# The second half of an output projection: four pairs in phases on four banks, their first phase laced with the first half's last pair

## The chip, the cores and the metric

The kernel runs on one core of one Trainium2 chip. The metric is the device time of one execution in microseconds (us), as the median of several runs; a profiled execution of the same program gives the trace that is read below.

## The reference, cut to what matters

The program is a trunk of two layers on 256 tokens of width 2048, all in float32. Each layer has one input projection, two kinds of attention (8 heads each), one output projection, and a gated feed-forward block, with a norm and a residual around each half.

```python
def hybrid_mixer(h, layer, w_in, w_o, ...):
    proj = h @ w_in                       # 2048 -> 12 blocks of 512 columns
    ...                                   # 8 stick-breaking heads, 8 differential heads
    mix = jnp.concatenate([o_sb.reshape(b, s, SB_WIDTH),
                           o_d.reshape(b, s, DIFF_V_WIDTH)], axis=-1)
    return mix @ w_o                      # (256 x 2048) @ (2048 x 2048): the change is here

for l in range(DEPTH):                    # DEPTH = 2
    h = rms_norm(x, pre_mix_norm[l])
    m = hybrid_mixer(h, l, w_in[l], w_o[l], ...)
    x = x + rms_norm(m, post_mix_norm[l])
    h = rms_norm(x, pre_ffn_norm[l])
    f = swiglu(h, w_gate[l], w_up[l], w_down[l])
    x = x + rms_norm(f, post_ffn_norm[l])
```

## The kernel before

**A product and its weights.** Every float32 weight block is split in two: ScalarE writes its rounded part `hi` (`activation ... Copy`), VectorE the rest `lo = w - hi`. A product of 128 tokens x 128 rows of K with 512 columns is three matmuls of 512 columns: `hi` by the rounded tokens, `lo` by the rounded tokens, `hi` by the tokens' rest (function `product`, and the same in `unit`). Weights arrive by DMA into `raw` (four buffers of 128 x 1024), in one order that is fixed when the kernel is built (`weight_order`); the split goes into `hi` and `lo` (six buffers each). What is to be split next stands in a list of jobs, which `weights` and `feed_jobs` work off a few jobs ahead of the product.

**A pair.** K is handled in pairs of 128-row blocks (`kp` = 0 to 7). The output projection has four blocks of 512 columns (`c` = 0 to 3), done as a first half (c = 0, 1) and a second half (c = 2, 3). With the two token blocks, two K blocks and two column blocks, one pair is a 2 x 2 by 2 x 2 product of blocks. There are three ways to do it:

- plain (`unit`): 8 products, 24 matmuls, two column blocks one after the other; VectorE makes one `lo` of 128 x 1024 for each column block;
- in seven (`mixed_weights`, `seven_products`): 7 products, 21 matmuls, after sums of weights (`t2`, `t3`, `t4`, ...) and sums of tokens (`pair_forms`, `token_sums`: tiles `sh`, `sl`); four of the products go into banks of their own (`p1`, `p6`, `p7`, `q5`), which are added to the results later, so eight banks are in use;
- phased (`phased`): the same 7 products for several pairs, but first the products `g0`, `t1`, `t2`, `t3` of all pairs into the four result banks, then four operations of VectorE and two copies of ScalarE that mix the banks, then `g1`, `b22`, `t4` of all pairs on top. Four banks are enough. The weight sums are made from three loads: `u1` (128 x 512 per pair), `first` (128 x 1024 per pair: a job that makes `g0` and `t1`, a job that makes `t2` and `t3`), `g1` (128 x 512 per pair, two pairs in a tile: the job for `g1`, then one for `b22` and `t4` of each pair). `first_part` and `second_part` do these jobs.

**The order.** TensorE (PE), VectorE (DVE) and ScalarE (ACT) each run their instructions in an order that is set when the kernel is built: a scheduler sets it from priorities (`tc.high_priority`, `tc.issue_after` pull things forward or hold them back), and in `passage`, the bridge from the output projection to the feed-forward block, it is written by hand. In the first half of the output projection pairs 4, 5, 6 are phased (`O_PHASED`) and pairs 7, 0, 2, 1, 3 plain (`O_PLAIN`). In the second half pairs 4 and 5 (`O_SEVEN`) are done in seven, with weights in buffers of their own (`V`), the other six plain; the last ones (`LATE_O[-1]`, `LAST_O`) are done in `passage`, one token block after the other, between the steps of the norm. While the plain pairs of the first half run, the attention's last heads are finished, and x and the norm's gain are loaded.

## Time and profile before

| | |
|---|---|
| time, median of 3 runs (lowest to highest) | 2169.59 us (2169.15 to 2169.59) |
| profiled execution: time, span of its instructions | 2169.97 us, 2168.3 us |
| PE busy, share of the span, instructions | 2154.1 us, 99%, 9896 |
| DVE busy, share, instructions | 1986.9 us, 92%, 2767 |
| ACT busy, share, instructions | 1434.7 us, 66%, 2163 |
| output projection: start of the first and of the last matmul, layer 1 of 2 | 297.8 us, 389.3 us |
| output projection: start of the first and of the last matmul, layer 2 of 2 | 1375.9 us, 1467.4 us |

Times count from the span's start. In the rows below a line number with an L is a line of the kernel, an arrow leads from the inputs to the output of an instruction, and brackets hold the time that the engine sat idle before it and what it waited for. DVE and matmul rows overlap a little: what an engine can do in a stretch is read from the distance of the starts, not from the durations. The lines of the changed kernel are numbered differently from those of the kernel before: of `first_part`, L354, L356 and L360 are now L352, L354 and L358; `lo = w - hi` (L346) is now L344; of `second_part`, L375 is now L373; the mixing in `phased`, L1222 to L1230, is now L1230 to L1238; the norm's gain, L703, is now L701.

### The profile page before, as it was taken

The numbers are of one execution on the slowest core, as the hardware profiler recorded it, in microseconds if no ns is written. First come the engines' busy times: TensorE is split into PE (matmuls) and PEld (weight loads), VectorE is DVE, ScalarE is ACT, GpSimd is POOL, SyncE is SP. The second block draws the span as 40 slices with busy tenths as digits, with TensorE's granted clock in tenths as the row PEclk, the third lists the DMA queues.
The fourth block names the chain that finished last, engine by engine and source line by source line (L and its number), as shares of the span: only waits on it lengthen the run. The fifth ranks groups of instructions, "written<-read, shape, count | busy, mean of one in ns | idle before, by whom it ended". The sixth has DMA issues, their size and how long they took to land.

```text
span 2168.3 us, 28898 instructions
## 1 busy us (share of the span) xinstructions
PE 2154.1 (99%) x9896; PEld 1773.9 (82%) x9896; DVE 1986.9 (92%) x2767; ACT 1434.7 (66%) x2163; POOL 241.1 (11%) x234
## 2 busy tenths in 40 slices
PE   9999999999999999999999999999999999999998
PEld 7888888888888888888878888888888888888887
DVE  7898987899999999999897989888999999999997
ACT  7667775766766666666575777757566666666664
POOL 1110000021221220000020100000112222100000
PEclk9999999999999999999999999999999999999999
DMA  8554556497887776777465555555978878767683
GB/s 295 183 193 157 173 175 246 156 309 235 243 264 224 233 240 226 227 228 253 147 207 188 176 182 175 182 204 190 308 218 269 242 224 241 230 218 245 201 270 99
DMA packets 143155, 470.43 MB, mean 217 GB/s; under 512 B 16272, under 2 KB 17296, under 8 KB 142496
## 3 DMA queue, kind: packets, MB, share of 16 engines
q1 hardware_dynamic: 124832, 436.03, 57.9%
q0 software_dynamic: 17600, 32.02, 9.0%
q8 instruction: 77, 1.26, 0.2%
q14 instruction: 70, 0.57, 0.1%
q10 hardware_dynamic: 576, 0.54, 0.1%
HBM read 460.14 MB, written 8.39 MB: 216 GB/s over the span
## 4 chain that ended last, share of the span: by engine, by line
PE 91%; DVE 4%; ACT 2%; DMA 2%; issue 1%; DVEq 0%; ACTq 0%
PE c L1311 21%; PE in L1255 5%; PE in L1254 5%; PE in L1256 5%; PE dn L1634 4%; PE dn L1631 4%; PE dn L1632 4%; PE p L1255 3%; PE p L1256 3%; PE c L1255 3%; PE c L1254 3%; PE c L1256 3%; PE p L1254 3%; DVE lo L346 2%; PE o L693 2%; PE o L695 2%
## 5 line engine op out<-in xcount | busy, mean ns | idle before, releaser
L346 DVE TENSOR_TENSOR lo<-raw,hi 128x1024 fp32r<-128x1024 f32 (+1 forms) x512 | 594.6, 1179 | 62.1 <-ACT hi L407 35.8
L407 ACT ACTIVATE hi<-raw 128x1024 fp32r<-128x1024 f32 x440 | 450.9, 1057 | 107.2 <-DMA raw<-in_weights_in_turn_dram 71.9
L1311 PE MATMUL c<-hi,xF 128*128 128x512 f32 x1344 | 364.3, 392 | 0.5 <-DVE xF L608 0.5
L1311 PEld LDWEIGHTS c<-hi,xF 128*128 128x128 f32 x1344 | 249.9, 188 | 52.6 <-DVE xF L608 1.3
L301 POOL DMA_DIRECT2D T<-in_weights_in_turn_dram x122 | 106.9, 876 | 1364.8 <-DMA T<-in_weights_in_turn_dram 279.2
L1311 PE MATMUL c<-lo,xF 128*128 128x512 f32 x672 | 207.5, 390 | 0.0
L322 ACT ACTIVATE Th<-T 128x512 fp32r<-128x512 f32 x122 | 77.2, 632 | 182.8 <-DVE T L333 180.6
L322 ACT ACTIVATE Th<-G 128x1024 fp32r<-128x1024 f32 x122 | 129.0, 1058 | 77.0 <-DVE G L334 75.8
L1631 PE MATMUL dn<-hi,jh 128*128 128x512 f32 x416 | 162.1, 390 | 0.0
L1632 PE MATMUL dn<-lo,jh 128*128 128x512 f32 x416 | 161.9, 389 | 0.0
L324 DVE TENSOR_TENSOR Tl<-G,Th 128x1024 fp32r<-128x1024 f32 x122 | 148.8, 1220 | 11.6 <-ACT Th L322 11.6
L407 ACT ACTIVATE hi<-G 128x1024 fp32r<-128x1024 f32 x122 | 129.0, 1057 | 41.6 <-DMA G<-in_weights_in_turn_dram 21.3
L324 DVE TENSOR_TENSOR lo<-T,hi 128x1024 fp32r<-128x1024 f32 x122 | 152.1, 1247 | 0.0
L334 DVE TENSOR_TENSOR G<-G,T 128x1024 f32<-128x1024 f32 x122 | 148.6, 1218 | 1.8
L1311 PEld LDWEIGHTS c<-lo,xF 128*128 128x128 f32 x672 | 126.0, 188 | 26.4
L346 DVE TENSOR_TENSOR lo<-G,hi 128x1024 fp32r<-128x1024 f32 x106 | 129.2, 1219 | 10.5 <-ACT hi L407 10.5
L322 ACT ACTIVATE hi<-T 128x1024 fp32r<-128x1024 f32 x122 | 128.1, 1050 | 12.0 <-PE c L1256 9.1
L1634 PE MATMUL dn<-hi,jl 128*128 128x512 f32 x416 | 128.2, 389 | 0.0
L1254 PE MATMUL in<-hi,xT 128*128 128x512 f32 x309 | 122.2, 398 | 0.8 <-ACT hi L1008 0.8
L1255 PE MATMUL in<-lo,xT 128*128 128x512 f32 x309 | 120.9, 392 | 1.4 <-DVE lo L346 1.4
L1256 PE MATMUL in<-hi,xT 128*128 128x512 f32 x309 | 120.3, 390 | 0.0
L1254 PE MATMUL in<-hi,xI 128*128 128x512 f32 x285 | 114.2, 401 | 0.0
(462 smaller groups left out, 5064.3 us busy)
## 6 DMA issues: line engine op xcount, KB each, us to landing
raw<-in_weights_in_turn_dram SPq DMA_DIRECT2D x510, 512.0 KB, 4.9
T<-in_weights_in_turn_dram SPq DMA_DIRECT2D x122, 512.0 KB, 5.3
G<-in_weights_in_turn_dram SPq DMA_DIRECT2D x122, 512.0 KB, 5.4
T<-in_weights_in_turn_dram POOLq DMA_DIRECT2D x122, 256.0 KB, 5.6
u<-in_weights_in_turn_dram SPq DMA_DIRECT2D x36, 256.0 KB, 5.7
V<-in_weights_in_turn_dram SPq DMA_DIRECT2D x8, 512.0 KB, 4.6
away_ffn<-x SPq DMA_DIRECT2D x8, 512.0 KB, 7.2
xd<-away_ffn SPq DMA_DIRECT2D x8, 512.0 KB, 8.7
```

What stands on the lines that cost most here:

```text
L322: nc.scalar.activation(h, w, AF.Copy)
L324: newest_rest[i] = nc.vector.tensor_tensor(out=l, in0=w, in1=h.bitcast(F32), op=ALU.subtract)
L334: nc.vector.tensor_tensor(out=g, in0=g, in1=t2.unsqueeze(1).to_broadcast([P, 2, CW]), op=ALU.add)
L346: rests.append(nc.vector.tensor_tensor(out=lo, in0=src, in1=hi.bitcast(F32), op=ALU.subtract))
L407: nc.scalar.activation(hi, raw, AF.Copy)
L1254: nc.tensor.matmul(a, sh, hi, start=first, stop=False, skip_group_check=open_sums[0])
L1255: nc.tensor.matmul(a, sh, lo, start=False, stop=False, skip_group_check=open_sums[0])
L1256: return nc.tensor.matmul(a, sl, hi, start=False, stop=last, skip_group_check=open_sums[0])
L1311: nc.tensor.matmul(a, stat[part], w[j][:, kk, :], start=first and kk + n == 0, stop=last and kk == 1 and n == 2)
L1631: nc.tensor.matmul(accs[c, t], sh, hi[:, kk, :], start=first, stop=False, skip_group_check=open_sums[0])
L1632: nc.tensor.matmul(accs[c, t], sh, lo[:, kk, :], start=False, stop=False, skip_group_check=open_sums[0])
L1634: nc.tensor.matmul(accs[c, t], sl, hi[:, kk, :], start=False, stop=last, skip_group_check=open_sums[0])
```

## The change

In the second half pairs 4, 5, 6 and 7 are phased (`O_LATER`), on four banks, in place of 4 and 5 in seven on eight banks; pairs 0, 1, 2, 3 are plain there, 1, 2 and 3 of them in `passage`. The first half's last plain pair, pair 3, is moved into the first phase of the second half: after the first products of pair 4 its column block 0, after those of pair 5 its column block 1. So two sets of four banks are open at once. The token sums of pairs 4 and 5 are still those made for the first half; those of pairs 6 and 7 are made once more (`later`), after two of the plain pairs of the first half. In `passage` the adding of the extra banks goes (one copy of ACT, eight additions of DVE).

```diff
-LATE_O = (6, 4, 0, 1, 5, 2)
-LAST_O = (3, 7)
-O_SEVEN = (4, 5)
+O_LATER = (4, 5, 6, 7)
+LATE_O = (0, 1)
+LAST_O = (2, 3)
...
-    def queue_phase(key, name, l, kps, cc):
+    def queue_phase(key, name, l, kps, cc, between=()):
+        between = list(between)
         for some in in_twos(kps):
             roles[queue(*((name, l, 2 * kp + 1, cc[1]) for kp in some))] = "u1", key, some
             for kp in some:
                 roles[queue(*((name, l, 2 * kp, c) for c in cc))] = "first", key, (kp,)
+                if between:
+                    between.pop(0)()
...
-        order_o = [(c, kp) for kp in O_PLAIN for c in (0, 1)]
-        order_o += [(c, kp) for kp in LATE_O for c in (2, 3)] + [(c, kp) for c in (2, 3) for kp in LAST_O]
+        for kp in O_PLAIN[:-1]:
+            for c in (0, 1):
+                queue_o(c, kp)
+        queue_phase(("o2", l), "w_o", l, O_LATER, (2, 3), [lambda c=c: queue_o(c, O_PLAIN[-1]) for c in (0, 1)])
+        for c, kp in [(c, kp) for kp in LATE_O for c in (2, 3)] + [(c, kp) for c in (2, 3) for kp in LAST_O]:
+            queue_o(c, kp)
...
+    def upper_room(key, name):          # where u1 of the new phase lies: in mg's second half, then in V's two buffers
+        if key[0] != "o2":
+            return late_room([P, 2, CW], name)
+        return spare_rooms.pop(0) if spare_rooms else mix_pool[0].tile([P, 2, CW], F32, tag="v", bufs=2, name=name)
...
-        for two in in_twos(kps[:-2]):
+        for two in in_twos(kps[:alone]) if not between else [(kp,) for kp in kps[:alone]]:
             for names in (("g0", "t1"), ("t2", "t3")):
                 for kp in two:
                     products(kp, *names)
+            if two[-1] in others:
+                place, work = others[two[-1]]
+                work()
...
         with tc.manual_schedule(engines=by_hand):     # passage
             last_units(0, (0, 1))
-            nc.scalar.copy(m[0], p1)
-            nc.vector.tensor_tensor(out=m[1], in0=p6, in1=m[0], op=ALU.subtract)
-            ...
+            if extra:                                 # None for the output projection now
+                ...
...
+            if n == 4:
+                for (later, tags, bufs) in zip(O_LATER[2:], (("ah", "al"), ("w", "w")), (1, 3)):
+                    forms[later] = pair_forms(pool, pool, bufs, mix, later, f"later{l}", tags=tags)
...
+        phased(got, forms, mix, ("o2", l), O_LATER, [w[0], w[1], w[0]], [lambda c=c: end_of_half(c) for c in (0, 1)])
         for kp in LATE_O[:-1]:
-            ...                                       # plain, or seven_products for O_SEVEN
+            for c in (2, 3):
+                unit({t: accs[c, t] for t in range(NT)}, mix, plan[l]["o"][c, kp], kp, range(NT), False, False)
```

The order of the instructions is the same in both kernels up to the last plain pairs of the first half; it differs from there to the end of `passage`, in each layer, on PE, DVE, ACT and the DMA queue of SyncE (SP), and nowhere else. In names such as `lo115_0`, 115 is the place of the load in the weights' order and 0 or 1 the job; `o0_2_1` is layer 0, column block 2, token block 1.

DVE where the second half begins, layer 0, before:

```order
L800 SCALAR_TENSOR_TENSOR mix_sb0_1_1_0_3385<-oT_ps_sb0_1_1_3387,gains_89,mix_sb0_1_1_0_3385 128x256
L346 TENSOR_TENSOR lo114_3382<-raw114_3379,hi114_3381 128x1024
L800 SCALAR_TENSOR_TENSOR mix_sb0_1_1_1_3386<-oT_ps_sb0_1_1_3387,gains_89,mix_sb0_1_1_1_3386 128x256
L346 TENSOR_TENSOR lo115_3411<-raw115_3408,hi115_3410 128x1024
L346 TENSOR_TENSOR lo116_3429<-V116_3426,hi116_3428 128x1024
L328 TENSOR_TENSOR V117_3450<-V116_3426,V117_3450 128x512
L324 TENSOR_TENSOR lo117_3453<-V117_3450,hi117_3452 128x1024
```

DVE at the same place now, from the plain tile `lo114` (pair 3, column block 0) to the second of pair 6's two first tiles:

```order
L344 TENSOR_TENSOR lo114_3413<-raw114_3410,hi114_3412 128x1024
L798 SCALAR_TENSOR_TENSOR mix_sb0_1_1_0_3416<-oT_ps_sb0_1_1_3418,gains_89,mix_sb0_1_1_0_3416 128x256
L352 TENSOR_TENSOR raw115_3439<-raw115_3439 128x512
L798 SCALAR_TENSOR_TENSOR mix_sb0_1_1_1_3417<-oT_ps_sb0_1_1_3418,gains_89,mix_sb0_1_1_1_3417 128x256
L354 TENSOR_TENSOR mg_o0_1_1_2956<-mg_o0_1_1_2956,raw115_3439 128x512
L352 TENSOR_TENSOR raw118_3488<-raw118_3488 128x512
L344 TENSOR_TENSOR lo115_0_3442<-raw115_3439,hi115_0_3441 128x1024
L344 TENSOR_TENSOR lo115_1_3466<-mg_o0_1_1_2956,hi115_1_3465 128x512
L358 TENSOR_TENSOR raw115_3439<-raw115_3439,mg_o0_1_1_2956 128x512
L344 TENSOR_TENSOR lo116_3475<-raw116_3472,hi116_3474 128x1024
L344 TENSOR_TENSOR lo115_1_3466<-raw115_3439,hi115_1_3465 128x512
L354 TENSOR_TENSOR u1_117_0_3484<-u1_117_0_3484,raw118_3488 128x512
```

Between two whole `lo` tiles there now stand additions of 128 x 512 for the phased pairs, and the addition that waits for `raw118` stands ahead of `lo115_0`.

DVE in the middle of the second half, layer 0, before (pair 5 in seven, after plain tiles):

```order
L346 TENSOR_TENSOR lo121_3538<-raw121_3535,hi121_3537 128x1024
L346 TENSOR_TENSOR lo122_3565<-V122_3562,hi122_3564 128x1024
L328 TENSOR_TENSOR V123_3580<-V122_3562,V123_3580 128x512
L324 TENSOR_TENSOR lo123_3583<-V123_3580,hi123_3582 128x1024
L333 TENSOR_TENSOR V123_3580<-V123_3580 128x512
L334 TENSOR_TENSOR V122_3562<-V122_3562,V123_3580 128x1024
```

DVE now, between the last product of the first phase and the first tile of the last phase (`lo120_0`, which PE reads for `g1`):

```order
L701 TENSOR_TENSOR mg_o0_0_0_2953<-o0_1_0_2950,gpost_mix0_3222 128x512
L701 TENSOR_TENSOR mg_o0_1_0_2954<-o0_1_1_2952,gpost_mix0_3222 128x512
L344 TENSOR_TENSOR lo119_1_3542<-raw119_3527,hi119_1_3541 128x512
L1230 TENSOR_TENSOR w0_o0_3463<-o0_3_1_3462,w0_o0_3463 128x512
L373 TENSOR_TENSOR mg_o0_0_1_2955<-raw120_3572,mg_o0_0_1_2955 128x512
L1234 TENSOR_TENSOR o0_2_1_3461<-o0_2_1_3461,w0_o0_3463 128x512
L1237 TENSOR_TENSOR o0_3_0_3460<-o0_3_0_3460,w0_o0_3463 128x512
L373 TENSOR_TENSOR mg_o0_1_1_2956<-raw120_3572,mg_o0_1_1_2956 128x512
L1238 TENSOR_TENSOR o0_3_1_3462<-o0_3_0_3460,w1_o0_3464 128x512
L344 TENSOR_TENSOR lo120_0_3575<-raw120_3572,hi120_0_3574 128x1024
```

The first half's gain, the mixing of the banks and the sums for the last phase all stand ahead of `lo120_0`.

PE in the second half, layer 0, before (the end of pair 4 in seven, then a plain pair):

```order
L1254 MATMUL p7_o0_3527<-Th117_3454,sho0_4_2782 128x512
L1255 MATMUL p7_o0_3527<-Tl117_3455,sho0_4_2782 128x512
L1256 MATMUL p7_o0_3527<-Th117_3454,slo0_4_2783 128x512
L693 MATMUL o0_2_0_3485<-hi118_3491,mix_sb0_0_0_0_3179 128x512
L694 MATMUL o0_2_0_3485<-lo118_3492,mix_sb0_0_0_0_3179 128x512
L695 MATMUL o0_2_0_3485<-hi118_3491,mix_sb0_0_0_0_3179 128x512
```

PE now, where the first phase ends and the last one begins:

```order
L1262 MATMUL o0_2_1_3461<-hi119_1_3541,shlater0_7_3387 128x512
L1262 MATMUL o0_2_0_3459<-hi120_0_3574,mix_df0_0_0_1526 128x512
L1263 MATMUL o0_2_1_3461<-lo119_1_3542,shlater0_7_3387 128x512
L1264 MATMUL o0_2_1_3461<-hi119_1_3541,sllater0_7_3388 128x512
L1262 MATMUL o0_2_1_3461<-hi121_1_3594,mix_df0_0_0_1526 128x512
L1262 MATMUL o0_3_0_3460<-hi121_1_3594,sho0_4_2782 128x512
L1263 MATMUL o0_2_0_3459<-lo120_0_3575,mix_df0_0_0_1526 128x512
L1264 MATMUL o0_2_0_3459<-hi120_0_3574,mix_df0_0_0_1526 128x512
```

Matmuls that need only `hi` (L1262) now stand ahead of those that wait for a `lo` (L1263) of an earlier product.

## The prediction

> **What bounds the kernel now.** I read the page first, then what PE waited for, then the timelines of PE and DVE around the change.

> ```profile
> span 2168.3 us, 28898 instructions
> PE 2154.1 (99%) x9896; PEld 1773.9 (82%) x9896; DVE 1986.9 (92%) x2767; ACT 1434.7 (66%) x2163; POOL 241.1 (11%) x234
> ...
> PE 91%; DVE 4%; ACT 2%; DMA 2%; issue 1%; DVEq 0%; ACTq 0%
> ...
> L407 ACT ACTIVATE hi<-raw 128x1024 fp32r<-128x1024 f32 x440 | 450.9, 1057 | 107.2 <-DMA raw<-in_weights_in_turn_dram 71.9
> ...
> raw<-in_weights_in_turn_dram SPq DMA_DIRECT2D x510, 512.0 KB, 4.9
> ```

> ```profile
> PE in L1255 <- DVE lo L346: 4.0, 8, 0.7
> PE c L1311 <- DVE xF L608: 0.5, 2, 0.2
> ```

> PE is the bound, with 91% of the chain that ended last. But DVE stands at 92%, so there is little of it left to spend, and the longest entry of PE's waits is PE waiting for a `lo` of DVE, eight times. All eight are in the input projection (`in`, L1255). So the question for each edit is: how many matmuls does it take from PE, and how much work does it give to DVE just where PE needs the results.

> The price of a matmul is the distance of two starts:

> ```profile
> 341.44 0.39 PE L693 MATMUL o<-hi,mix_sb 128*128 128x512 f32 x1
> 341.67 0.39 PE L694 MATMUL o<-lo,mix_sb 128*128 128x512 f32 x1
> ...
> 346.88 0.39 PE L693 MATMUL o<-hi,mix_df 128*128 128x512 f32 x1
> ```

> From 341.44 to 346.88 are 24 matmuls, 0.227 us each, with no bracket in between: PE has no wait at all here. In the order, 341.44 is where the second half's first product stands in the changed kernel (the place after `lo111`'s last matmul, equal in both).

> The price of DVE's work, and what happens when it is late, is shown by a phased stretch of four pairs in the input projection, the nearest thing to the new one:

> ```profile
> 249.83 0.68 DVE L346 TENSOR_TENSOR lo<-u,hi 128x512 fp32r<-128x512 f32 x1
> 250.43 0.68 DVE L360 TENSOR_TENSOR raw<-raw,u 128x512 f32<-128x512 f32 x1
> 251.03 1.82 DVE L346 TENSOR_TENSOR lo<-raw,hi 128x1024 fp32r<-128x1024 f32 x2
> ...
> 258.38 1.22 DVE L346 TENSOR_TENSOR lo<-raw,hi 128x1024 fp32r<-128x1024 f32 x1
> 259.52 0.69 DVE L1226 TENSOR_TENSOR in<-in,w 128x512 f32<-128x512 f32 x1
> 260.12 1.21 DVE L346 TENSOR_TENSOR lo<-u,hi 128x1024 fp32r<-128x1024 f32 x1
> ```

> ```profile
> 251.16 0.40 PE L1254 MATMUL in<-hi,xT 128*128 128x512 f32 x1
> 252.30 0.50 PE L1255 MATMUL in<-lo,xT 128*128 128x512 f32 x1 [0.74 <-DVE lo L346]
> 252.64 0.39 PE L1256 MATMUL in<-hi,xT 128*128 128x512 f32 x1
> 252.87 0.39 PE L1254 MATMUL in<-hi,shin 128*128 128x512 f32 x1
> ```

> By the starts a DVE instruction of 128 x 512 takes 0.60 us (249.83 to 250.43 to 251.03), one of 128 x 1024 takes 1.14 (258.38 to 259.52); one that reads and writes a bank, 259.52 to 260.12, is 0.60 too. DVE has no bracket: it runs without a pause, and PE stands at 252.30 until the `lo` begun at 251.03 is written. That is the mechanism on which this prediction rests.

> The smaller forms, and where DVE stands ahead of the second half, in layer 0 and then in layer 1:

> ```profile
> 271.40 0.41 DVE L1064 TENSOR_TENSOR fo<-mix_df 128x256 f32<-128x256 f32 x1
> 271.73 1.22 DVE L346 TENSOR_TENSOR lo<-raw,hi 128x1024 fp32r<-128x1024 f32 x1
> ...
> 275.44 0.28 DVE L1263 TENSOR_TENSOR so<-fo 128x128 f32<-128x128 f32 x1
> 275.64 0.28 DVE L1262 TENSOR_TENSOR so<-so,fo 128x128 f32<-128x128 f32 x1
> ```

> ```profile
> 328.26 0.69 DVE L779 TENSOR_TENSOR on_sb<-o_sb,ors_sb 128x512 f32<-128x512 f32 x1
> 330.47 1.22 DVE L346 TENSOR_TENSOR lo<-raw,hi 128x1024 fp32r<-128x1024 f32 x1 [1.52 <-ACT hi L407]
> 331.61 0.48 DVE L800 SCALAR_TENSOR_TENSOR mix_sb<-oT_ps_sb,gains,mix_sb 128x256 fp32r<-128x256 f32 x1
> 332.01 1.21 DVE L346 TENSOR_TENSOR lo<-raw,hi 128x1024 fp32r<-128x1024 f32 x1
> ...
> 341.39 1.22 DVE L346 TENSOR_TENSOR lo<-raw,hi 128x1024 fp32r<-128x1024 f32 x1 [1.42 <-ACT hi L407]
> 344.00 1.22 DVE L346 TENSOR_TENSOR lo<-V,hi 128x1024 fp32r<-128x1024 f32 x1 [1.39 <-ACT hi L407]
> ...
> 1406.32 0.69 DVE L779 TENSOR_TENSOR on_sb<-o_sb,ors_sb 128x512 f32<-128x512 f32 x1
> 1407.55 1.23 DVE L346 TENSOR_TENSOR lo<-raw,hi 128x1024 fp32r<-128x1024 f32 x1 [0.53 <-ACT hi L407]
> ```

> ```profile
> 1419.51 0.39 PE L693 MATMUL o<-hi,mix_sb 128*128 128x512 f32 x1
> ```

> So 128 x 256 costs 0.33, 128 x 128 costs 0.20, the rest of `mix_sb` (L800) 0.40. The `lo` at 330.47 is `lo109`, the one at 1407.55 its counterpart in layer 1; 1419.51 is the counterpart of 341.44. DVE still idles here (1.42, 1.39): the plain stretch leaves it room.

> **The change part by part, per layer.**

> *Matmuls.* Four pairs in 7 products instead of two: 2 products x 3 matmuls fewer, 6 x 0.227 = -1.36 us. PE has nothing else to lose or win: the counts of its order differ by 12 in both layers together. -2.7 us for the program, all of it on the path.

> *DVE's work in the new stretch.* In DVE's order, from the first addition of pair 4 (L352 on `raw113`) to the last tile of the last phase (`lo121_4`) stand 53 instructions: 33 of 128 x 512, 12 of 128 x 1024, 2 of 128 x 256, 4 of 128 x 128, 2 `mix_sb`. That is 19.8 + 13.7 + 0.7 + 0.8 + 0.8 = 35.7 us. By purpose: the four pairs' weights 25.8 (per pair 3 additions and 2 half rests of 0.60 and a whole rest of 1.14; then 0.60 + 0.57 for `g1` and 1.14 for `b22`, `t4`), the four mixings of banks 2.4, the first half's gains 2.4, the two laced tiles 2.3, pair 7's token sums made again 2.1, `mix_sb` 0.8.

> *PE's work in the same stretch.* 28 products and the laced pair are 108 matmuls; `lo121_4` is read by the 103rd, so PE would come to it 102 x 0.227 = 23.1 us after 341.44. DVE needs 12.6 us more than PE for the stretch.

> *DVE's lead.* Ahead of the 53 stand, from 330.47: `lo109`, `mix_sb`, one form of 128 x 128, `lo110`, `mix_sb`, one of 128 x 512, `lo111`: 1.14 + 0.40 + 0.20 + 1.14 + 0.40 + 0.60 + 1.14 = 5.0, done at 335.5. The other four of pair 6's token sums (2 x 0.33 + 3 x 0.20 = 1.3) go ahead of `lo109`, into its bracket of 1.52: I cost them at nothing. So DVE starts 5.9 us ahead of PE. In layer 1 the bracket is only 0.53, so they end at 1406.32 + 0.60 + 1.26 = 1408.2, `lo111`'s counterpart at 1413.2, 6.3 ahead of 1419.51.

> *The wait.* 35.7 - 23.1 - 5.9 = 6.7 us of lateness at `lo121_4`. Walking both orders tile by tile, PE first waits a little at `lo115_1` (349.5 against 349.4) and `lo118_1`, is 0.9 late at `lo119_0`, 2.0 at `lo119_1`, 5.9 at `lo120_0` (364.3 against 358.5: gains, mixing and sums are queued ahead of it) and 6.9 at `lo121_1` (367.8 against 360.9), the most; behind it, at 1.14 us a tile, DVE keeps pace, and in the plain pair that follows (1.14 for 12 matmuls, 2.7 us) it draws ahead. So +6.9 in layer 0, +6.5 in layer 1, if DVE itself never waits: 13.4.

> *DVE's own waits.* A rounding takes ACT 1.06 us (L407 on the page) and stands between two steps of DVE; the order mostly puts other work in between. One load is tight: `raw118` reuses `raw113`, free when DVE is done with it at about 341.1, and its addition stands in DVE's queue at 344.8, with `lo115_0`, for which PE waits, behind it. By the page's median from issue to landing, 4.9, it lands at 346.0, 1.2 late; if it takes under 3.7 it is in time. How full the DMA is there:

> ```profile
> 321.00:337.00 16.00, 16.00 (x82) 13.20 (x81) 9.86 (x19) 10.22 (x30) 0.00 (x0) 1.00 0.88 321
> 337.00:352.00 15.00, 15.00 (x68) 12.42 (x67) 10.31 (x14) 7.61 (x15) 0.00 (x0) 1.00 0.65 241
> ```

> The share falls from 0.88 (x and the gain are loaded there) to 0.65 in the stretch of that load. Bounds 0 and 1.5 per layer; I take 0.6, in the lower half for that share: 1.2 for both. The loads of `u1` for pairs 4 and 5 now stand among those of the plain tiles; they go into free rooms, 256 KB each: nothing, and if that cover is gone they delay `lo109`, which is inside the 1.5.

> *What goes in `passage`.* One copy of ACT and eight additions of DVE, 4.8 us.

> ```profile
> 395.43 0.87 DVE L608 SCALAR_TENSOR_TENSOR xF<-xT_ps,gains,xF 128x128 fp32r<-128x128 f32 x3 [1.35 <-ACT xF L600]
> ```

> DVE waits there for ACT (1.35), not ACT for it, and PE's wait behind it is 0.5 in all (L608 among PE's waits). I cost this at nothing; at most it gives back those 0.5. If DVE's backlog reached into `passage` it would cost more, but eight tiles of 1.14 from 371.2 on are done at 380.3, and PE comes to `passage` 156 matmuls after 341.44 and 6.9 late, at 383.8.

> *Sum.* -2.7 + 13.4 + 1.2 = +11.9 us. The profiled execution took 2169.97 us, so 2181.9; the median of the runs shown is 0.4 lower, so **2181.5**.

> [...]

> **The rivals.**

> 1. *PE doesn't wait, and the change does what the six matmuls say*: 2169.6 - 2.7 = 2166.9. For it: the plain stretch before leaves DVE idle (1.42, 1.39 and 1.52 in the rows), and in the input projection the eight waits cost only 4.0 visible. Against it: there the attention's matmuls fill PE between the products, here no attention is left; and it needs a lead of 5.9 + 6.9 = 12.8 us. It decides at that figure: `lo111` would have to be done at 328.6, before `lo109`, two tiles ahead of it, could start (330.47, behind ACT). 6%.
> 2. *Half of the lead is found* (the first half's DVE work runs earlier than in the trace, or PE itself comes later): a wait of about 1.4 us a layer would just take back the gain, 2169 to 2170. It needs a lead of 11.4. 5%.
> 3. *DVE waits for loads and ACT as well*: at the bound of 1.5 a layer and more, since each stall of DVE holds a `raw` buffer longer and so the next load: 2184 to 2188. For it: `raw118`. Against it: all later loads have 4 us and more between their buffer's release and their use. 9%.
> 4. *PE runs slower after its waits.* After the wait of 0.74 the next start comes 0.34 later, the one after that 0.23, the old pace. My longest single waits are about 2 us, two of them between `lo119_1` and `lo120_0`, with matmuls that need only `hi` in between. If PE ran at half pace for as long as it had waited, 3.5 us a layer would be added: about 2188. 2%. [...]

> **How the numbers follow.** My forecast, the wait for DVE at its computed size (2178 to 2185: the sum with 0 and with 1.5 us of DVE's own waits, and 0.5 for `passage`), has 78%. Rivals 3 and 4 are slower too: slower 89%, faster 6%, same 5%. A change under 0.2% (4.3 us) can't be told from none. The range is to hold 8 times in 10: the forecast's own, widened to 2175 below (a layer with 2 us more lead) and to 2187 above (rival 3).

> **What would show it.** The page after: some 12 fewer PE instructions, PE's busy time no longer 99% in the second half, DVE without a bracket from about 330.5 to 371 and from 1408 to 1449, PE's waits naming `o` L1263 and DVE `lo` L344 with the largest before `lo120_0`, the bridge's first matmuls about 6 us later than before in layer 0. I would be wrong if DVE showed brackets there while PE ran through (lead or order misread), or if PE waited for a DMA or for ACT instead.

## The result and the profile after

The changed kernel takes 2184.31 us (median of 4 runs, 2183.07 to 2187.37); the kernel before, beside it, 2169.59 (4 runs, 2169.15 to 2173.51). The ratio is 1.0065, 95% interval 1.0053 to 1.0078: slower by 0.65%. Forecast were 2181.5 us and a range of 2175 to 2187.

The page of the profiled execution after (2185.25 us):

```profile
span 2183.4 us, 28955 instructions
PE 2162.1 (99%) x9884; PEld 1775.2 (81%) x9884; DVE 2005.6 (92%) x2819; ACT 1446.6 (66%) x2181; POOL 240.6 (11%) x234
...
PE 83%; DVE 10%; ACT 3%; DMA 2%; issue 2%; DVEq 0%; ACTq 0%
```

PE has 12 instructions fewer and is still busy longer. DVE's share of the chain that ended last rose from 4% to 10%, PE's fell from 91% to 83%.

Where the 15.28 us between the two profiled executions lie, read from the first and last matmul of the output projection (`o`) in PE's timeline:

| | before | after | difference |
|---|---|---|---|
| program start to the first `o` matmul, layer 0 | 297.81 | 299.46 | +1.65 |
| `o`, layer 0, first to last matmul | 91.50 | 99.36 | +7.86 |
| `o`, layer 1, first to last matmul | 91.49 | 97.81 | +6.32 |
| all the rest | | | -0.55 |

The first row is not the change: no instruction differs there, and in the profiles of the experiments it lies between 297.18 and 300.76. What causes this scatter was not looked into. So the change costs 14.2 us, and the length of `o`, which this scatter does not touch, is the measure used below. It is read from one profiled execution of each kernel.

What PE waited for there, by the list of waits of the whole run (us in total, times, longest), and then the timelines of PE, DVE and ACT in layer 0:

```profile
PE o L1262 <- ACT hi L379: 3.3, 2, 1.6
PE o L1262 <- DVE o L1238: 2.1, 2, 1.1
PE o L1263 <- DVE lo L344: 1.0, 2, 0.6
```

```profile
361.88 0.40 PE L1264 MATMUL o<-hi,sllater 128*128 128x512 f32 x1
363.91 0.50 PE L1262 MATMUL o<-hi,mix_df 128*128 128x512 f32 x1 [1.63 <-ACT hi L379]
365.48 0.80 PE L1262 MATMUL o<-hi,sho 128*128 128x512 f32 x1 [1.07 <-DVE o L1238]
366.61 0.79 PE L1263 MATMUL o<-lo,mix_df 128*128 128x512 f32 x1 [0.33 <-DVE lo L344]
367.20 0.63 PE L1264 MATMUL o<-hi,mix_df 128*128 128x512 f32 x1
367.62 0.63 PE L1262 MATMUL o<-hi,mix_df 128*128 128x512 f32 x1
368.05 0.63 PE L1263 MATMUL o<-lo,mix_df 128*128 128x512 f32 x1
```

```profile
337.26 0.68 DVE L352 TENSOR_TENSOR raw<-raw 128x512 f32<-128x512 f32 x1
...
359.61 1.28 DVE L701 TENSOR_TENSOR mg_o<-o,gpost_mix 128x512 f32<-128x512 f32 x2
360.81 0.68 DVE L344 TENSOR_TENSOR lo<-raw,hi 128x512 fp32r<-128x512 f32 x1
361.41 0.68 DVE L1230 TENSOR_TENSOR w_o<-o,w_o 128x512 f32<-128x512 f32 x1
362.01 0.68 DVE L373 TENSOR_TENSOR mg_o<-raw,mg_o 128x512 f32<-128x512 f32 x1
362.93 0.70 DVE L1234 TENSOR_TENSOR o<-o,w_o 128x512 f32<-128x512 f32 x1 [0.24 <-ACT w_o L1233]
...
365.34 1.21 DVE L344 TENSOR_TENSOR lo<-raw,hi 128x1024 fp32r<-128x1024 f32 x1
...
373.35 1.21 DVE L344 TENSOR_TENSOR lo<-raw,hi 128x1024 fp32r<-128x1024 f32 x1
```

```profile
362.31 0.58 ACT L1233 COPY w_o<-o 128x512 f32<-128x512 f32 x1 [1.36 <-PE o L1264]
362.80 1.06 ACT L379 ACTIVATE hi<-mg_o 128x1024 fp32r<-128x1024 f32 x1
364.91 1.06 ACT L379 ACTIVATE hi<-mg_o 128x1024 fp32r<-128x1024 f32 x1 [1.05 <-DVE mg_o L373]
```

PE runs three matmuls between 361.88 and 366.61. DVE runs from 337.26 to 373.35 with a single bracket, 0.24. The list of waits names ScalarE first, with 3.3 us; but the rounding at 362.80 needs DVE's addition of 362.01 (L373), done at 362.69, and stands in ScalarE's queue behind a copy that waits for PE's matmul of 361.88, the last of the product that reads DVE's `lo` of 360.81. Both that `lo` and the addition stand behind the gains (L701) in DVE's queue. The next rounding carries a bracket that names DVE itself. Wait lists show the last link; here the first link is the backlog of DVE.

Then something that the waits don't show: from 367.20 the matmuls stand 0.43 apart instead of 0.227. The granted clock, in steps of 3.41 us (columns: busy time and instructions of PE, PEld, DVE, ACT, POOL, then PEclk, DMA share, GB/s), layer 0 and then layer 1:

```profile
358.47:361.89 3.42, 3.05 (x11) 1.72 (x10) 3.42 (x7) 2.49 (x4) 0.00 (x0) 1.00 0.27 102
361.89:365.30 3.41, 0.89 (x3) 0.19 (x1) 3.17 (x6) 1.93 (x3) 0.00 (x0) 1.00 0.42 154
365.30:368.71 3.41, 2.90 (x6) 2.01 (x7) 3.41 (x5) 2.14 (x3) 0.00 (x0) 0.50 0.34 102
368.71:372.13 3.42, 3.42 (x9) 2.62 (x9) 3.42 (x4) 1.92 (x3) 0.00 (x0) 0.50 0.55 205
372.13:375.54 3.41, 3.41 (x16) 2.80 (x16) 3.41 (x4) 2.76 (x3) 0.00 (x0) 1.00 0.00 0
...
1447.33:1450.74 3.41, 1.00 (x2) 0.37 (x2) 3.23 (x5) 2.15 (x3) 0.00 (x0) 1.00 0.32 130
1450.74:1454.15 3.41, 2.97 (x7) 2.36 (x8) 3.41 (x5) 2.34 (x3) 0.00 (x0) 0.50 0.41 154
1454.15:1457.57 3.42, 3.42 (x16) 2.80 (x16) 3.42 (x4) 2.73 (x3) 0.00 (x0) 1.00 0.46 153
```

Behind a step in which PE ran two or three matmuls, where 15 fit, the clock is 0.50: for two steps in layer 0, for one in layer 1.

### The profile page after: what moved, and what is told of

Same layout as the page of the kernel before. It is cut to its first block, busy times and chain, and to the rows that moved or that the text cites. A ratio compares the mean times of both kernels' runs of the same rounds, so it can differ in the third digit from the quotient of the medians.

```text
span 2183.4 us, 28955 instructions
## 1 busy us (share of the span) xinstructions
PE 2162.1 (99%) x9884; PEld 1775.2 (81%) x9884; DVE 2005.6 (92%) x2819; ACT 1446.6 (66%) x2181; POOL 240.6 (11%) x234
## 3 DMA queue, kind: packets, MB, share of 16 engines
q8 instruction: 77, 1.26, 0.2%
## 4 chain that ended last, share of the span: by engine, by line
PE 83%; DVE 10%; ACT 3%; DMA 2%; issue 2%; DVEq 0%; ACTq 0%
PE c L1320 21%; PE in L1263 5%; PE in L1264 5%; PE in L1262 5%; DVE lo L344 5%; PE dn L1649 4%; PE dn L1652 4%; PE dn L1650 4%; PE p L1263 3%; PE c L1263 3%; PE c L1262 3%; PE p L1264 3%; PE c L1264 3%; PE p L1262 3%; DMA raw<-in_weights_in_turn_dram 2%
## 5 line engine op out<-in xcount | busy, mean ns | idle before, releaser
L344 DVE TENSOR_TENSOR lo<-raw,hi 128x1024 fp32r<-128x1024 f32 (+1 forms) x524 | 605.1, 1172 | 61.0 <-ACT hi L405 32.8
L405 ACT ACTIVATE hi<-raw 128x1024 fp32r<-128x1024 f32 x432 | 443.3, 1057 | 110.6 <-DMA raw<-in_weights_in_turn_dram 74.1
L1320 PE MATMUL c<-hi,xF 128*128 128x512 f32 x1344 | 364.3, 392 | 0.5 <-DVE xF L606 0.5
L323 ACT ACTIVATE Th<-G 128x1024 fp32r<-128x1024 f32 x122 | 129.0, 1057 | 76.7 <-DVE G L332 75.5
L405 ACT ACTIVATE hi<-G 128x1024 fp32r<-128x1024 f32 x122 | 129.0, 1057 | 40.6 <-DMA G<-in_weights_in_turn_dram 19.1
L344 DVE TENSOR_TENSOR lo<-G,hi 128x1024 fp32r<-128x1024 f32 x106 | 129.2, 1219 | 10.2 <-ACT hi L405 10.2
L1262 PE MATMUL in<-hi,xT 128*128 128x512 f32 x309 | 123.1, 401 | 0.8 <-DVE xT L979 0.8
L1263 PE MATMUL in<-lo,xT 128*128 128x512 f32 x309 | 121.3, 394 | 0.5 <-DVE lo L344 0.5
L1262 PE MATMUL in<-hi,xI 128*128 128x512 f32 x285 | 114.1, 400 | 0.0
## 6 DMA issues: line engine op xcount, KB each, us to landing
raw<-in_weights_in_turn_dram SPq DMA_DIRECT2D x514, 512.0 KB, 4.7
T<-in_weights_in_turn_dram SPq DMA_DIRECT2D x122, 512.0 KB, 5.2
G<-in_weights_in_turn_dram SPq DMA_DIRECT2D x122, 512.0 KB, 5.4
away_ffn<-x SPq DMA_DIRECT2D x8, 512.0 KB, 7.3
xd<-away_ffn SPq DMA_DIRECT2D x8, 512.0 KB, 8.1
```

Source lines behind the costliest of these rows:

```text
L323: nc.scalar.activation(h, w, AF.Copy)
L344: rests.append(nc.vector.tensor_tensor(out=lo, in0=src, in1=hi.bitcast(F32), op=ALU.subtract))
L405: nc.scalar.activation(hi, raw, AF.Copy)
L1262: nc.tensor.matmul(a, sh, hi, start=first, stop=False, skip_group_check=open_sums[0])
L1263: nc.tensor.matmul(a, sh, lo, start=False, stop=False, skip_group_check=open_sums[0])
L1320: nc.tensor.matmul(a, stat[part], w[j][:, kk, :], start=first and kk + n == 0, stop=last and kk == 1 and n == 2)
```

## The experiments

Two questions: is the loss the amount of DVE's work, and what does the half clock cost?

**Matmuls that keep PE busy while it waits.** In `phased`, for the new phase:

```diff
+        if between:
+            fill = acc_bank(...)
+            for _ in range(12):
+                nc.tensor.matmul(fill, tiles[2 * kps[-1]][:, 0, 0:P], blocks[key, kps[-1]]["t3"][0], start=True, stop=True)
         for kp in kps:
             products(kp, "g1")
```

> The changed kernel with 12 more matmuls (128 x 512, into a free bank, results unused) in PE's order at the place of its longest waits, between the first phase and g1. They take 2.7 us of a stretch in which PE has 0.45 us of work in 4.7 us. DVE's work and order are the same. The measure is the output projection from its first to its last matmul, 99.36 us in layer 0 and 97.81 in layer 1 of the changed kernel (91.50 and 91.49 before). Theory: the granted clock falls to 0.50 because PE does almost nothing in a stretch of 3.4 us; with the matmuls it stays at 1.00, and the stretch shortens by what the half pace cost beyond DVE's lateness. Placing the same tiles of DVE behind each other, PE at full pace would meet DVE again at the next two tiles, so that is 1.3 us in layer 0 and about 0 in layer 1: 98.1 and 97.8, time about 2183. Rival 1, the half pace costs all that its intervals show (2.6 and 1.4 us): 96.8 and 96.4, time about 2180. Rival 2, the low clock has another cause than PE's idleness: clock 0.50 again, 99.4 and 97.8, 2184.

Measured: `o` 97.53 us in layer 0 and 97.27 in layer 1, that is -1.83 and -0.54; 2182.22 us, ratio to before 1.0054 (1.0039 to 1.0070). The clock stays at 1.00:

```profile
362.40:365.81 3.41, 2.19 (x9) 1.31 (x8) 3.41 (x6) 1.69 (x3) 0.00 (x0) 1.00 0.13 52
365.81:369.22 3.41, 2.72 (x12) 1.85 (x12) 3.41 (x4) 3.19 (x4) 0.00 (x0) 1.00 0.74 208
```

So PE's idleness caused the half clock, and the half clock cost some 2.4 us in both layers together: more than the replayed 1.3 and less than the 4 us that the longer intervals show, since at full pace PE meets DVE's next tile again (1.22 us at 365.06, 0.69 at 367.40). One reservation: DVE's addition of L1234 stands one place later here, its 0.24 of waiting is gone, and up to that much per layer may belong to it and not to the clock.

**The gains behind the last phase.** `gained(...)` of the first half is called after the plain pair that follows the last phase, not in `end_of_half`:

> The changed kernel with the four gain multiplications of the first half (128 x 512, 0.60 us each) behind the last phase instead of ahead of it in DVE's queue; nothing else moves. Theory (PE's lateness is DVE's backlog of work up to the last phase's tiles): 2.4 us less per layer, and where that brings PE's two long waits down, no half clock in layer 0 either (up to 1.3 more): output projection 95.7 to 97.0 us in layer 0 and 95.4 in layer 1, time 2178 to 2179.5. Rival (the wait hangs on ScalarE's rounding, which the list of PE's waits names with 3.3 us, or on a load): no change, 99.4 and 97.8, 2184.

Measured: 96.23 and 94.72, -3.13 and -3.09; 2180.28 us, ratio 1.0045 (1.0031 to 1.0059). That is the 2.4 us and what the clock gave back: layer 1 has no half clock any more, layer 0 one step of it instead of two (mean granted clock of the profiled execution 0.998, against 0.997). Layer 1 came out 0.7 below the stated 95.4, where no gain from the clock had been counted, and the time 0.8 above the stated range. PE's waits in `o` no longer name ScalarE's L379. The amount of DVE's work ahead of the tiles sets the time; the rival falls.

**The lacing undone.** The first half ends with pair 3, then the four pairs are phased without lacing:

> The changed kernel without the lacing: the first half ends with its pair 3 as before, then the four pairs are phased, the last two of them product by product in turn. The work of every engine is the same, only its order differs. Theory (PE's lateness is the sum of VectorE's work up to the last phase's tiles, less its lead): the sum is the same, so the output projection stays within 1 us of 99.4 and 97.8 us, time 2182 to 2186. Rival (the lacing, with its two sets of open banks and its gains ahead of the last phase, makes the wait): at least half of the loss comes back, 95.5 or less in layer 0, time 2177 or less.

Measured: 97.81 and 97.13, -1.55 and -0.68; 2181.71 us, 1.0049 (1.0035 to 1.0062). In layer 0 this is more than the stated 1 us, and the time lies just under the theory's range; the rival's 95.5 is far off. One step of half clock is left in layer 0, none in layer 1 (mean granted clock 0.998, against 0.997), which by the first experiment accounts for most of it. With gains and token sums moved (below), undoing the lacing made `o` longer:

> Both moves, gains and token sums, and no lacing. Without the moves, undoing the lacing gave 1.55 and 0.68 us, most of it in layer 0 where one stretch of half clock was left of two. Theory: with the moves no half clock is left to save, the sum of VectorE's work is the same as in the laced kernel with the moves: 93.0 to 94.0 us, time 2175 to 2177. Rival (the lacing itself costs about 0.7 us a layer): 92.3 to 93.0.

Measured: 94.21 and 93.89, layer 0 a little above the theory's range and layer 1 in it, against 93.64 in both with the lacing; 2174.67 us, 1.0022 (1.0013 to 1.0031). The lacing is not the cause of the loss.

**Token sums on GpSimd.** In `pair_forms` and `token_sums`, `nc.gpsimd` instead of `nc.vector` for pairs 6 and 7 of the second half:

> The changed kernel with the token sums of pairs 6 and 7 (for the second half alone) made by GpSimd instead of VectorE: per layer seven instructions a pair, 2.1 us of VectorE's time for pair 7 within the stretch and 0.8 us of pair 6's ahead of it; pair 6's others stood in an idle bracket of VectorE. Theory (amount of DVE work): 2.9 us less per layer, and the half clock of layer 0 gone or shorter: output projection 95.2 to 96.5 and 94.9, time 2177 to 2178.5. Rival 1 (GpSimd's instructions hold up VectorE's while they run): VectorE's additions take more than 0.60 us beside GpSimd's, and less than half of the 2.9 us comes back, 2181 to 2184. Rival 2 (ScalarE or loads set the wait): no change, 2184.

Measured: 102.52 and 102.98, +3.2 and +5.2; 2193.42 us, 1.0108 (1.0094 to 1.0121). Worse than any rival; the clock is at 0.50 for two steps in layer 0 and for three in layer 1 (mean granted clock 0.995, against 0.997). ScalarE's queue, and DVE behind it:

```profile
338.45 0.63 ACT L1282 ACTIVATE shlater<-slater 128x512 fp32r<-128x512 f32 x1 [3.63 <-POOL slater L1274]
```

```profile
340.06 1.47 DVE L344 TENSOR_TENSOR lo<-raw,hi 128x1024 fp32r<-128x1024 f32 x1 [4.08 <-ACT hi L405]
```

GpSimd's sums are late; ScalarE waits 3.63 us to round them, and behind that rounding in its queue stands `hi` of a plain tile, for which DVE then waits 4.08. So one late engine stopped two others through a queue.

**All three moves of DVE's work**: gains late, token sums on GpSimd, and the four additions of L373 on GpSimd:

> The changed kernel with three moves of VectorE's work in each layer: the first half's gains behind the last phase (2.4 us), the token sums of pairs 6 and 7 on GpSimd (2.9 us), and the four additions that prepare the last phase's sums (128 x 512) on GpSimd (2.4 us). Theory: the backlog of 8.0 us in layer 0 and 7.7 in layer 1 shrinks by 7.7, PE hardly waits, the clock stays at 1.00, and what is left is the six matmuls saved: output projection 90.2 to 91.2 us in both layers, time 2167 to 2169, 0.02 to 0.1% under the kernel before. Rival 1 (GpSimd takes about twice as long and its result comes too late for the tiles of the last phase, or holds up VectorE): waits for GpSimd of 1 to 3 us a layer, 2171 to 2175. Rival 2 (the change has another cost than VectorE's backlog): 2175 or more.

Measured: 100.41 and 99.86; 2189.19 us, 1.0085 (1.0071 to 1.0099; one of the five runs took 7740 us, which is not in the ratio and was not explained). The late sums act as above, and the additions show rival 1 at its plainest, GpSimd first, then DVE beside it:

```profile
354.40 3.40 POOL L373 TENSOR_TENSOR mg_o<-raw,mg_o 128x512 f32<-128x512 f32 x2 [16.19 <-DMA raw<-in_weights_in_turn_dram]
```

```profile
354.86 1.79 DVE L344 TENSOR_TENSOR lo<-u,hi 128x512 fp32r<-128x512 f32 x1
356.57 1.77 DVE L358 TENSOR_TENSOR raw<-raw,u 128x512 f32<-128x512 f32 x1
358.27 0.68 DVE L354 TENSOR_TENSOR u<-u,raw 128x512 f32<-128x512 f32 x1
```

Beside GpSimd's two additions of 1.70 us, DVE's two of 0.60 take 1.71 and 1.70. The other two additions of this layer, at 358.48 and 363.06, do the same: the DVE instructions beside them take 2.23 instead of 1.14 (from 358.87) and 1.68 instead of 0.60 (from 364.04). DVE saves 0.60 per addition moved and loses 1.1.

**Gains late, token sums earlier on DVE.** The sums of pairs 6 and 7 are made after the third plain tile instead of the fifth (`if n == 2`), in DVE's idle time:

> The changed kernel with the gains behind the last phase (as in the run before, which measured 96.2 and 94.7 us) and the token sums of pairs 6 and 7, on VectorE again, two plain tiles earlier, where VectorE stood idle for 2.5 us waiting for ScalarE. Theory: of the sums 2.0 to 2.9 us leave the path of VectorE's backlog: output projection 93.3 to 94.2 in layer 0 and 91.8 to 92.7 in layer 1, time 2174.5 to 2176.5. Rival (the earlier sums only push the plain tiles back, since the idle time there is set by ScalarE's order): 96 and 94.5, 2180.

Measured: 93.64 in both layers; 2175.67 us, 1.0024 (1.0015 to 1.0033). Layer 0 as expected, layer 1 shorter by 1.1 instead of 2 to 2.9; why less came back there was not tested (layer 0 also had a step of half clock to lose). No half clock any more (mean granted clock 0.999, as in the kernel before). 2.1 us a layer above the kernel before.

**Besides, the additions of L373 by accumulating DMAs**:

```diff
+                if key[0] == "o2":
+                    nc.gpsimd.dma_start(t2, stream[i][:, j, :], accum_op=ALU.add)
+                    continue
                 nc.vector.tensor_tensor(out=t2, in0=raw[:, j, :], in1=t2, op=ALU.add)
```

> The same, and besides the four additions that prepare the last phase's sums (128 x 512, 2.4 us of VectorE per layer) made by accumulating DMAs of 256 KB that GpSimd issues, instead of by VectorE or by GpSimd's own arithmetic, beside which VectorE's 128 x 512 took 1.7 us instead of 0.60. Theory: 2.4 us less of backlog: output projection 90.9 to 91.8 and 90.2 to 90.6, time 2169 to 2172, about the kernel before. Rival 1 (the accumulation lands after the tiles are due; the kernel's other loads of this kind take 5.8 us from issue to landing): PE or ScalarE waits for the DMA, 2174 to 2178. Rival 2 (issuing on GpSimd holds VectorE up as its arithmetic does): VectorE's additions longer than 0.60 us, 2176 or more.

Measured: 95.43 and 95.00; 2180.36 us, 1.0042 (1.0028 to 1.0055). Rival 1:

```profile
365.26 0.80 PE L694 MATMUL o<-hi,mix_sb 128*128 128x512 f32 x1 [2.99 <-ACT hi L408]
```

```profile
363.20 1.06 ACT L382 ACTIVATE hi<-u 128x1024 fp32r<-128x1024 f32 x1 [2.52 <-issue]
364.16 1.99 ACT L408 ACTIVATE hi<-raw 128x1024 fp32r<-128x1024 f32 x2
```

The rounding of pair 7's sum stands still for 2.52 us. The profile names no releaser for it; the accumulation, issued at 356.01, is the one input still missing, so this is inferred. PE does not need that rounding yet: it waits for the one queued behind it, and the clock falls to 0.50 again for one step (mean granted clock 0.998). DVE's instructions of 128 x 512 keep their 0.60 here, so rival 2 falls.

**Eight of DVE's additions left out** (L352 and L373 of the new phase), on top of gains late and sums earlier:

> The kernel with gains and token sums moved (output projection 93.64 us in both layers) without eight of VectorE's weight additions of the phase per layer: the four that make t1 and the four that prepare the last phase (128 x 512, 4.8 us together) are left out, so these products use unsummed weights; every matmul stays. Theory (VectorE's backlog, 3.5 us by PE's gaps there, is all that the six saved matmuls are missing): the backlog is gone, the output projection is 1.36 us shorter than before's 91.50, with at most 0.7 us of waiting for the mixing of the banks: 90.1 to 90.9 us, time 2167 to 2168.5. Rival (PE has waits of its own in the phases, for the mixing, ScalarE's roundings or loads, that do not shrink with VectorE's load): 92 us or more, 2171 or more.

Measured: 90.30 and 90.09; 2167.70 us, 0.9986 (0.9977 to 0.9995). This kernel leaves out part of the weight sums, so its results are not the layer's: it measures, and is no version to use. In the stretch of `o` PE's list of waits is empty. With 4.8 us less of DVE's work the six matmuls are worth just what their count says: -1.20 and -1.40 against -1.36 a layer.

**Fewer pairs.** Two pairs (4, 5), no lacing:

> Only pairs 4 and 5 phased in the second half, without lacing; pairs 6, 7, 0 to 3 plain. The matmuls are as many as in the kernel before (two pairs in seven products), no token sums are made again, and the eight additions of the bridge are gone. Theory: VectorE has 20.9 us of work (13.0 for two pairs, 2.4 mixing, 2.4 gains, 2.3 for pair 3, 0.8 mix_sb) against 14.9 us of PE's, and a lead of 6: PE is hardly late, output projection 91.3 to 92.5 us, time 2169 to 2171. Rival (phasing on four banks costs PE its own wait for the mixing of the banks, whatever VectorE's load): 93 to 94.5 us, time 2173 to 2175.

Measured: 94.38 and 92.90; 2174.65 us, 1.0015 (1.0006 to 1.0024). The theory's number was missed, most in layer 0, and the time is the rival's (2173 to 2175): there PE's starts are late by 0.3 to 0.8 us at four places, in layer 1 by 0.2 to 0.7 at three. In layer 0 DVE had lost time before, to a load:

```profile
341.00 0.69 DVE L352 TENSOR_TENSOR raw<-raw 128x512 f32<-128x512 f32 x1 [2.20 <-DMA raw<-in_weights_in_turn_dram]
```

In layer 1 this bracket is 0.5; the 1.7 between the two is about the difference between the layers (1.5). The other 1.4 us are PE's waits where the phases change, for the mixing of the banks and for the `lo` tiles queued around it. A sum of work does not contain these: they come from the order of DVE's instructions there, with gains and mixing between the tiles. That is read from the rows and was not tested by itself. The mixing alone does not make them: with the gains late and without the eight additions (above) the banks are mixed too, and PE waits for nothing. Three pairs, laced, with both moves:

> Both moves, with three pairs phased (4, 5, 6) instead of four; laced. Three matmuls fewer than before per layer instead of six, and 6.5 us less work for VectorE against 4.8 us less for PE in the stretch. Theory: lateness 1.9 us instead of 3.5: output projection 92.2 to 92.9 us, time 2171.5 to 2174. Rival 1 (what PE waits for in two pairs, the mixing and a late load, is there with three too and does not fall with VectorE's work): 93.5 to 94.5. Rival 2 (lateness gone altogether): 90.8, time 2168.

Measured: 91.42 and 91.27; 2171.72 us, 1.0003 (0.9994 to 1.0012): no difference to the kernel before that could be measured, and no version that computes everything was found to beat it. The wait is about 0.5 us instead of the 1.9 expected.

## Why the prediction was right, point by point

The direction was right, and so was the mechanism: DVE's work, queued ahead of the tiles that PE needs, is late by about the computed amount. One term was missing, the half clock, and the time lies in the range although it was left out: the forecast's own band, up to 2185, held only because it left room for 1.5 us a layer of DVE's own waits, and of these only 0.24 came. That part is luck.

- *Matmuls, -2.7*: right, by the run without the additions.
- *DVE's 53 instructions, 35.7 us*: from 337.26 to 373.35 they took 36.1, with the 0.24 of waiting.
- *The lead*: `lo111` was to be done at 335.5, 337.15 on the clock of the changed kernel (its program start is 1.65 later); the addition behind it starts at 337.26. PE's first product of the second half starts at 343.05, so the lead was 5.8 instead of 5.9.
- *The wait for DVE, 6.9 and 6.5 with 0.6 of DVE's own waits each, together 7.5 and 7.1*: with the clock kept full, `o` is 97.53 and 97.27; less before's 91.50 and 91.49, and with the 1.36 of the saved matmuls, that is 7.4 and 7.1 us of lateness.
- *The price of an instruction*: the distance of the starts was the better one. With the durations, 0.68 in place of 0.60 and 1.22 in place of 1.14, each of the 53 would have cost some 0.08 more: an estimate of 40 us instead of the 36.1 measured.
- *DVE's own waits*: the 0.6 was right in size by chance. The addition on `raw118` shows no bracket, the load came in time; in its place stand 0.24 (ACT's copy) and, in layer 0, 0.34 of PE's for `mix_sb`. The 0.24 is gone in the run with the fill, from which the 7.4 and 7.1 are taken; what makes up the rest of their distance to 6.9 and 6.5 was not traced.
- *The names of the waits*: wrong, and PE waiting for ACT had been called a sign that the prediction fails. `lo` was to be named most; the list names ScalarE's `hi` (3.3) and the mixing (2.1) ahead of it (1.0), because PE's order puts products that need a `hi` of the next phase ahead of `lo120_0`. What ACT waits for there is DVE's backlog: with the gains moved behind the tiles, that wait leaves the list. The times of DVE's tiles were right: the 53 were to end at 371.2, which is 372.85 on this clock, and ended at 373.35.
- *`passage`, 0 to -0.5*: from the first to the last matmul behind it, the gate and up products take 460.35 instead of 460.89 us in layer 0 and 461.43 instead of 461.38 in layer 1. That agrees, but shows little: the same stretch takes 460.40 to 461.83 in the experiments.
- *Rival 4, half pace after the waits, at 2%*: this is what the prediction had wrong. In the kernel before, the old pace of 0.23 was back one start after a wait of 0.74; here the waits came as two of 1.6 and 1.1 us with one matmul between them, and the clock was 0.50 behind them, the matmuls 0.43 apart. It cost about 2.4 us by the fill experiment, 1.8 in layer 0 and 0.5 in layer 1 and not the 3.5 a layer of the rival's own price, since PE at full pace would have met DVE's next tile again. Without it the lateness of 14.5 less the 2.7 of the matmuls leaves 11.8, against the 11.9 forecast.
- *Rivals 1 to 3*: no lead was found, and loads did not come late in the changed kernel.

## What to carry to other kernels

Before PE's time is bought with DVE's work, add up what DVE has to do in that stretch, from the start-to-start times of its rows, and set it against PE's time there plus DVE's lead: here DVE was busy for 92% of the span, but in the stretch it had 36 us of work where PE's time and the lead gave it 29. Work that nobody waits for (here the gains) belongs behind the tiles that somebody waits for; handing it to GpSimd did not help here, since its additions held DVE up (1.1 us for 0.60 saved) and its sums came late in a queue that DVE needs. And where PE has to wait for several microseconds, what it does in between counts too: here twelve idle matmuls kept its clock at 1.00, and `o` was 1.83 and 0.54 us shorter.

## What the runs showed of the hardware

```profile
344.93:348.35 3.42, 1.75 (x8) 1.08 (x6) 3.42 (x6) 1.23 (x3) 0.00 (x0) 1.00 0.45 148
348.35:351.76 3.41, 2.76 (x12) 2.34 (x13) 3.26 (x6) 2.65 (x3) 0.00 (x0) 1.00 0.71 274
...
1433.79:1437.20 3.41, 1.30 (x6) 0.75 (x4) 3.41 (x6) 1.36 (x3) 0.00 (x0) 1.00 0.39 130
1437.20:1440.61 3.41, 3.17 (x8) 2.53 (x9) 3.26 (x6) 2.49 (x4) 0.00 (x0) 0.50 0.59 235
```

- Beside GpSimd's additions DVE did not get slower by a share: in layer 0 each of the four put it back by the same 1.1 us, whether DVE's own instruction takes 0.60 (1.71, 1.70, 1.68) or 1.14 (2.23). Why was not shown.
